# Attention with relative-position tables: the tables of a unit's two heads side by side and loaded in one transfer, queries as one run per partition

## The chip, the cores and the metric

The kernel runs on one core of one Trainium2 chip. The metric is the device time of one execution in microseconds. Before the change it is 1325.63 us, the median of three runs (1324.44 to 1329.54). A profile of one execution comes with it. Its engines are called PE (TensorE, matrix multiplication), DVE (VectorE), ACT (ScalarE), POOL (GpSimd) and SP (SyncE, which in this kernel issues most of the transfers); each issues its instructions in order, and the transfers that it issues form a queue of their own.

## The reference, cut to what matters

One layer over 2048 tokens (a grid of 32 rows by 64 columns) of width 1024. One in-projection makes the inputs of two branches, whose outputs lie beside each other and go through one out-projection.

```python
def hybrid_mixer(h, w_in, b_in, conv_w, conv_b, rpb, ml_norm_w, w_out):
    proj = h @ w_in + b_in
    (na_q, na_k, na_v, na_z, ml_q, ml_k, ml_v, ml_o, ml_z,
     i_f, f_f, i_b, f_b) = jnp.split(proj, split_idx, axis=-1)
    na_out = neighbourhood_attention(na_q, na_k, na_v, rpb) * jax.nn.silu(na_z)
    qk = jax.nn.silu(centred_short_conv(jnp.concatenate([ml_q, ml_k], axis=-1), conv_w, conv_b))
...
    # attention: each of 8 heads, each query: 8 rows x 16 columns of keys around it
    bias = rpb[:, dy[:, None, :, None], dx[:, None, :, None]]
    s = jnp.einsum('bhrcd,bhrjkd->bhrcjk', qg, kg).astype(jnp.float32) + bias[None]
    s = jnp.where(col_mask[:, None, :], s, -jnp.inf)
    p = jax.nn.softmax(s.reshape(B, NA_HEADS, rows, GRID_W, kh * GRID_W), axis=-1).reshape(s.shape)
    o = jnp.einsum('bhrcjk,bhrjkd->bhrcd', p, vg)
...
    return jnp.concatenate([na_out, ml_out], axis=-1) @ w_out
...
    # the layer
    h = rmsnorm(h_res, norm_w[l]) * (1.0 + scale[:, None, :]) + shift[:, None, :]
    h_res = h_res + gate[:, None, :] * y
    return rmsnorm(h_res, final_norm_w).astype(x.dtype)
```

The second branch is a bidirectional mLSTM of 4 heads, whose queries and keys pass the short convolution. The bias depends only on where a key lies relative to its query, and on the edges of the grid.

## The kernel before, in words

Everything is float32. A weight or an activation that goes through PE is split into a high and a low part, and a product is three matmuls (high by high, low by high, high by low). The work lies in stages one after the other:

- the start and the token blocks (to about 329 us): the norm, the values of both branches, the gates and decays of the mLSTM;
- the convolution stage, `conv_blocks` (329 to 519 us): the keys and queries of the mLSTM, four weight blocks of eight tiles each. A tile is 24 matmuls on PE into PSUM; ACT evicts it to a tile `u` (L891, four buffers); DVE convolves `u` into a tile `acc` in five instructions (L926, L928, five buffers); ACT applies SiLU (L930); SP stores `acc` to `d_ck` (L933). For keys, PE also transposes `acc` (L939, `kt`), ACT scales the result into `stk` (L941), and SP stores it (L943). Between tiles the generator `gated_out` prepares the out-projection's weights: SP loads a piece `wraw` (L854), DVE multiplies it by the gate (L861), SP stores it to `d_wo` (L862);
- the queries and keys of the attention (L986, PE's `pq`) and the mLSTM (to about 960 us);
- phase 2, the attention and the out-projection (to the end).

**The bias tables** are made by transfers alone. `tables_begin` fills the small tensors `d_e` in DRAM with a large number, `tables_columns` copies the bias of each column into them (L648, 48 transfers), `table_fills` fills the tables `d_t`, and `tables_rows` (L670) copies eight rows of `d_e` for each of eight grid rows into `d_t`, DRAM to DRAM, on SP. There are nine tables, three kinds of patch rows by three kinds of patch columns, with eight `tables_rows` copies each, 72 in all. `conv_blocks` calls `tables_rows` three times at the head of each of its first three weight blocks; each copy takes the eight heads as its first dimension.

**Phase 2** goes by units. The grid is cut into 16 patches of 8 rows by 16 columns (128 queries), and a unit is a patch with two of its heads: 64 units, taken two at a time. For a unit PE multiplies queries and keys (L1477), DVE adds the table and takes the minimum along the row in one instruction per head (L1485), ACT takes the exponent (L1486), DVE normalises (L1497), PE transposes the weights (L1505), ACT copies them out of PSUM (L1507), and PE multiplies them with the values (L1520). The out-projection's matmuls (L1565) lie between. A unit's tables lie in SBUF in `tabs`, two places of two tiles; neighbouring units of like patches share a place, and when a unit is the last user of its place, its minimum is followed by the load of the next unit's table, per head:

```python
                    if u in follows:
                        load_tab(follows[u], j)
```

`load_tab` (L1449) issues on SP, but for the first two units on POOL; `load_q` (L1392) loads the queries of two units, which were stored to `d_qna` in the stage before (L1025 and what follows).

**What sets the order.** Outside phase 2's hand-written schedule a scheduler orders each engine's instructions by its own estimate of when they are ready. So a change of a transfer's shape can move others.

## Time and profile before

| what | value |
|---|---|
| time, median of three runs | 1325.63 us (1324.44 to 1329.54) |
| span of the profiled execution | 1326.9 us |
| PE busy | 1294.6 us, 98% |
| DVE, ACT, POOL busy | 59%, 41%, 17% |
| SP's queue q1, share of 16 DMA engines over the span | 50.7% |
| start and token blocks, PE busy | 323.6 of 329 us |
| convolution stage (329 to 519 us), PE busy | 186.2 of 190 us, DMA share 0.64 |
| attention's queries and keys, mLSTM (519 to 960 us), PE busy | 436.9 of 441 us, DMA share 0.63 |
| phase 2 (960 to 1327 us), PE busy | 347.9 of 367 us, DMA share 0.74 |

The profiled execution's own time is its span, 1326.9 us, 1.3 us above the median of the runs. Rows of the timeline give start, duration, engine, line, instruction, output and inputs, and in brackets the idle time ahead of it with what ended it. On SP a row is an issue: its duration is the time SP took to hand the transfer over, not the transfer's. `x24` means that 24 such rows in a row are shown as one. A row of the table by windows gives the window, its length, the busy time of PE, PE's weight loads, DVE, ACT and POOL with the number of instructions, PE's granted clock (1.00 is full speed), the busy share of the 16 DMA engines and what they moved in GB/s.

### The profile page before, as it was taken

Reading aid. Unit: us, or ns where it says so; the run is one execution under the profiler, and the core shown is the slowest. Engines: PE = TensorE matmul, PEld = TensorE weight load, DVE = VectorE, ACT = ScalarE, POOL = GpSimd, SP = SyncE. Lnnn points to the kernel's source line nnn. Section 1 sums busy time; section 2 is a strip of 40 time slices with the busy share of each in tenths; the row PEclk is TensorE's granted clock in tenths of the full one; section 3 lists DMA queues with packets and bytes.
Section 4 is the critical chain, followed back from the end, with each engine's and each line's share of the span. In section 5 each row is a group of like instructions: output and inputs, shape, how many; then the busy total and the mean of one; then the engine's idle time right before and its main releaser. Section 6 shows DMA issues by size and latency. Waiting matters only on the chain. (4 is left out here: it accounts for less than half of the span.)

```text
span 1326.9 us, 23404 instructions
## 1 busy us (share of the span) xinstructions
PE 1294.6 (98%) x8330; PEld 1115.4 (84%) x8330; DVE 779.6 (59%) x2406; ACT 542.8 (41%) x1184; POOL 225.1 (17%) x280
## 2 busy tenths in 40 slices
PE   9999999999999999999999999999999999999996
PEld 8899999999878787888888888888777778778785
DVE  5754452112455559176768878767547576666663
ACT  5643324543222323123324323333356555565551
POOL 0243103331000000012212002121202211212211
PEclk9999999999999999999999999999999999999999
DMA  9998657998267685545756866746689977868871
GB/s 325 323 281 180 169 141 171 214 244 217 82 149 208 142 209 165 159 120 167 204 165 196 254 187 204 237 141 188 198 256 239 212 184 190 195 175 194 195 186 48
DMA packets 240487, 255.91 MB, mean 193 GB/s; under 512 B 31079, under 2 KB 200295, under 8 KB 240371
## 3 DMA queue, kind: packets, MB, share of 16 engines
q1 hardware_dynamic: 157006, 182.98, 50.7%
q0 software_dynamic: 20496, 36.21, 11.2%
q10 hardware_dynamic: 62868, 35.22, 9.6%
q8 instruction: 66, 1.08, 0.4%
q14 instruction: 51, 0.41, 0.1%
HBM read 169.81 MB, written 92.72 MB: 198 GB/s over the span
## 5 line engine op out<-in xcount | busy, mean ns | idle before, releaser
L986 PE MATMUL pq<-hhi,whi_a 128*128 128x512 f32 x512 | 208.2, 407 | 0.8 <-ACT u L891 0.8
L986 PE MATMUL pq<-hlo,whi_a 128*128 128x512 f32 x512 | 208.4, 407 | 0.0
L986 PE MATMUL pq<-hhi,wlo_a 128*128 128x512 f32 x512 | 206.7, 404 | 0.0
L986 PEld LDWEIGHTS pq<-hhi,whi_a 128*128 128x128 f32 x512 | 96.8, 189 | 17.8 <-ACT u L891 1.3
L986 PEld LDWEIGHTS pq<-hhi,wlo_a 128*128 128x128 f32 x512 | 96.8, 189 | 16.3
L986 PEld LDWEIGHTS pq<-hlo,whi_a 128*128 128x128 f32 x512 | 96.7, 189 | 16.0 <-issue 0.5
L1507 ACT ACTIVATE pt<-pT 96x384 f32<-96x384 f32 (+3 forms) x128 | 65.8, 514 | 86.7 <-PE pT L1505 84.0
L1486 ACT ACTIVATE pbuf<-pbuf,mn 128x480 f32<-128x480 f32 (+5 forms) x128 | 76.0, 594 | 53.0 <-DVE mn L1485 53.0
L960 POOL TENSOR_TENSOR wlo_a<-rawq,whi_a 128x1024 fp32r<-128x1024 f32 x19 | 45.8, 2409 | 296.1 <-ACT whi_a L959 263.7
L1565 PE MATMUL y<-hhi,whi_a 128*128 128x512 f32 x256 | 91.4, 419 | 0.5 <-ACT whi_a L1535 0.5
L1565 PE MATMUL y<-hhi,wlo_a 128*128 128x512 f32 (+1 forms) x272 | 90.7, 399 | 0.2 <-ACT y L1572 0.2
L1485 DVE CUSTOM_DVE_ANT_0 pbuf<-pS,tab 128x480 f32<-128x480 f32 (+5 forms) x128 | 62.9, 540 | 39.1 <-PE pS L1477 32.1
L1230 ACT ACTIVATE num<-px,gtile 128x129 f32<-128x129 f32 x120 | 38.3, 366 | 111.3 <-PE px L1225 86.5
L1505 PEld LDWEIGHTS pT<-ident,pbuf 128*128 128x128 f32 (+2 forms) x416 | 51.0, 137 | 29.6 <-issue 9.9
L618 DVE TENSOR_TENSOR stvo<-pvo,brow 128x256 f32<-128x256 f32 x64 | 26.6, 422 | 83.1 <-PE pvo L548 65.7
L1505 PE MATMUL pT<-ident,pbuf 128*128 128x128 f32 (+2 forms) x416 | 67.3, 275 | 8.2 <-DVE pbuf L1497 6.8
L546 PE MATMUL pvo<-whi_b,hhi 128*128 128x256 f32 x256 | 72.6, 284 | 0.0
L548 PE MATMUL pvo<-whi_b,hlo 128*128 128x256 f32 x256 | 72.1, 281 | 0.0
L547 PE MATMUL pvo<-wlo_b,hhi 128*128 128x256 f32 x256 | 72.0, 281 | 0.0
L1249 POOL TENSOR_TENSOR hm<-hm,ck 128x128 f32<-128x128 f32 x64 | 26.5, 414 | 252.9 <-DVE hm L1248 223.9
L833 ACT ACTIVATE dec<-dec,gtile 128x128 f32<-128x128 f32 x128 | 42.7, 393 | 53.6 <-POOL dec L826 50.8
L581 DVE TENSOR_TENSOR stv<-pv,brow 128x256 f32<-128x256 f32 x32 | 12.4, 421 | 74.4 <-DMA d_vna<-stv 43.4
(302 smaller groups left out, 3408.3 us busy)
## 6 DMA issues: line engine op xcount, KB each, us to landing
ck<-d_ck SPq DMA_DIRECT2D x64, 384.5 KB
rawq<-in_w_main_dram SPq DMA_DIRECT2D x28, 512.0 KB
raw<-in_w_main_dram SPq DMA_DIRECT2D x20, 512.0 KB
d_ck<-stvo SPq DMA_DIRECT2D x16, 514.0 KB
kv<-d_ck SPq DMA_DIRECT2D x64, 128.5 KB
wada<-in_w_ada_dram SPq DMA_DIRECT2D x32, 256.0 KB
dec<-d_mneg SPq DMA_DIRECT2D x32, 256.0 KB
d_ck<-dec ACTq DMA_DIRECT2D x32, 256.0 KB
```

The source lines that it names most:

```text
L546: nc.tensor.matmul(ps, lhi(k), rhi(k), start=(k == 0), stop=False)
L547: nc.tensor.matmul(ps, lhi(k), rlo(k), start=False, stop=False)
L548: self.mark = nc.tensor.matmul(ps, llo(k), rhi(k), start=False, stop=(k == KT - 1))
L833: nc.scalar.activation(t[:, o, :], t[:, o, :], AF.Exp, bias=self.cols["g"][:, d, h, c : c + 1])
L960: (eng or nc.gpsimd).tensor_tensor(lo[:, :, cs], raw, hi[:, :, cs].bitcast(F32), ALU.subtract)
L986: self.mark = nc.tensor.matmul(patch_ps(ps) if patch else ps, w, self.htok(h, g, k, patch), start=(k == 0 and n == 0), stop=(k == KT - 1 a ...
L1230: nc.scalar.activation(num[:, d, :], px[:, d, :], AF.Copy, scale=self.cols["inter"][:, d, h, c : c + 1])
L1485: nc.vector.tensor_tensor_reduce(pt[:, :nk], ps, tabs[place[u]][j][:, :nk], 1.0, 3e38, ALU.add, ALU.min, mn)
L1486: nc.scalar.activation(pt[:, :nk], pt[:, :nk], AF.Exp, bias=mn, scale=-1.0, accum_out=sums[:, j : j + 1])
L1505: nc.tensor.transpose(ps[:cs, i, :], U[u][j][:, i * cs : (i + 1) * cs], self.ident)
L1507: nc.scalar.activation(t[:cs, :nch, :], ps[:cs, :nch, :], AF.Copy)
L1565: nc.tensor.matmul(y, m[:, k, :], w[k][:, cs], start=(k == 4 and n == 0), stop=(k == 3 and n == 2))
```

## The change

Three layouts change, in DRAM and in SBUF.

- `d_e` and `d_t`, which held the 8 heads outermost, hold the 4 head pairs outermost; the two heads of a pair lie beside each other in a row. The copies of L648 and L670 follow: their access pattern begins with 4 instead of 8, and its second dimension is twice as long. Bytes and runs of each copy are the same.
- A unit's two tables are one SBUF tile of 960 columns instead of two of 480, and `load_tab` loads both in one transfer. It is issued once, behind the second head's minimum, where before each head's minimum was followed by its own load. SP issues 52 such transfers instead of 104, POOL 2 instead of 4.
- `d_qna` holds the queries of two units so that a partition reads one run of 2 KB instead of two of 1 KB. Their stores write runs of 512 bytes as before.

```diff
--- before.py
+++ after.py
@@ -98,7 +98,7 @@
         self.d_mneg = d.tile([P, CH], F32, name="d_mneg")
         self.d_zna = d.tile([16, P, 4, P], F32, name="d_zna")
         self.d_zml = d.tile([16, P, 4, P], F32, name="d_zml")
-        self.d_qna = d.tile([2, 2, 16, P, 2, P], F32, name="d_qna")
+        self.d_qna = d.tile([2, 16, P, 2, 2, P], F32, name="d_qna")
         self.d_kna = d.tile([2, 512, T], F32, name="d_kna")
         self.d_mix = d.tile([16, P, 4, P], F32, name="d_mix")
         self.d_wo = d.tile([KT, P, D], F32, name="d_wo")
@@ -106,9 +106,9 @@
         self.d_gate = d.tile([1, D], F32, name="d_gate")
         self.d_rneg = d.tile([NH, 15, 31], F32, name="d_rneg")
         nks = [24, 32, 24]
-        self.d_e = [d.tile([NH, 16, 15, nks[t]], F32, name=f"d_e{t}") for t in range(3)]
+        self.d_e = [d.tile([NH // 2, 16, 2, 15, nks[t]], F32, name=f"d_e{t}") for t in range(3)]
         nrs = [11, 15, 12]
-        self.d_t = [[d.tile([NH, P, nrs[r] * nks[t]], F32, name=f"d_t{r}{t}") for t in range(3)] for r in range(3)]
+        self.d_t = [[d.tile([NH // 2, P, 2, nrs[r] * nks[t]], F32, name=f"d_t{r}{t}") for t in range(3)] for r in range(3)]
 
     def constants(self):
         nc, c = self.nc, self.const
@@ -634,7 +634,7 @@
         nc.sync.dma_start(self.d_rneg.rearrange("h a b -> (h a) b"), r)
         for e in self.d_e:
             n = e.shape[-1] * 15 // 2
-            dst = e.rearrange("h c a k -> (h c) (a k)").rearrange("p (j n) -> p j n", j=2)
+            dst = e.rearrange("h c e a k -> (h c e) (a k)").rearrange("p (j n) -> p j n", j=2)
             nc.sync.dma_start(dst, self.big[:, :n].unsqueeze(1).broadcast_to([P, 2, n]))
 
     def tables_columns(self, ct):
@@ -645,7 +645,7 @@
             c = c0 + i
             start = min(max(c - 8, 0), GRID_W - 16)
             dx = start - c + 15
-            nc.sync.dma_start(self.d_e[ct][:, i, :, start - k0 : start - k0 + 16], self.d_rneg[:, :, dx : dx + 16])
+            nc.sync.dma_start(self.d_e[ct][:, i, :, :, start - k0 : start - k0 + 16].rearrange("h e a k -> h (e a) k"), self.d_rneg.rearrange("(h e) a k -> h (e a) k", e=2)[:, :, dx : dx + 16])
 
     def table_fills(self):
         nc = self.nc
@@ -653,7 +653,7 @@
             for rt in range(3):
                 t = self.d_t[rt][ct]
                 n = t.shape[-1]
-                dst = t.rearrange("h q k -> (h q k)").rearrange("(p j k) -> p j k", p=P, j=16)
+                dst = t.rearrange("h q e k -> (h q e k)").rearrange("(p j k) -> p j k", p=P, j=16)
                 nc.sync.dma_start(dst, self.big[:, : n // 2].unsqueeze(1).broadcast_to([P, 16, n // 2]))
                 yield
 
@@ -668,8 +668,8 @@
             dy = start - row + 7
             j0 = (start - PR_R0[pr]) * nk
             nc.sync.dma_start(
-                t[:, r * 16 : (r + 1) * 16, j0 : j0 + 8 * nk],
-                self.d_e[ct][:, :, dy : dy + 8, :].rearrange("h c a k -> h c (a k)"),
+                t[:, r * 16 : (r + 1) * 16, :, j0 : j0 + 8 * nk].rearrange("h q e n -> h (q e) n"),
+                self.d_e[ct][:, :, :, dy : dy + 8, :].rearrange("h c e a k -> h (c e) (a k)"),
             )
 
 
@@ -1022,7 +1022,7 @@
                 for e, part in enumerate((hv, lv)):
                     src = part.bitcast(F32).rearrange("p (a q) -> p a q", a=4)
                     if kind == "q":
-                        dst = self.d_qna[e, ct // 2, 4 * g : 4 * g + 4, :, ct % 2].rearrange("a p q -> p a q")
+                        dst = self.d_qna[ct // 2, 4 * g : 4 * g + 4, :, e, ct % 2].rearrange("a p q -> p a q")
                     else:
                         dst = self.d_kna[e, ct * P : (ct + 1) * P, g * GT : (g + 1) * GT].rearrange("p (a q) -> p a q", a=4)
                     late.append((dst, src))
@@ -1389,7 +1389,7 @@
             if 2 * i >= NU:
                 return
             b, c0 = units[2 * i][0], min(units[2 * i][1], units[2 * i + 1][1])
-            (nc.gpsimd, nc.gpsimd, nc.scalar, nc.sync)[min(i, 3)].dma_start(qs[i % 3].bitcast(F32), self.d_qna[:, c0 // 2, b].rearrange("e p c q -> p e c q"))
+            (nc.gpsimd, nc.gpsimd, nc.scalar, nc.sync)[min(i, 3)].dma_start(qs[i % 3].bitcast(F32), self.d_qna[c0 // 2, b])
 
         def load_v(b, most=4, queue=nc.gpsimd):
 
@@ -1434,7 +1434,7 @@
             L[b]["x"] = [x[:, 512 * i : 512 * i + 512] for i in range(2)]
             L[b]["row"] = x
 
-        tabs = [[p.tile([P, 480], F32, name=f"tab{i}{j}") for j in range(2)] for i in range(2)]
+        tabs = [p.tile([P, 960], F32, name=f"tab{i}") for i in range(2)]
         place, follows, user = [], {}, {}
         for u, (b, ct) in enumerate(units):
             same = [w for w in (u - 1, u - 3) if w >= 0 and units[w][1] == ct and units[w][0] != b and kind(units[w][0]) == kind(b)]
@@ -1443,10 +1443,11 @@
                 follows[user.get(place[u], -1 - place[u])] = u
             user[place[u]] = u
 
-        def load_tab(u, j):
+        def load_tab(u):
             b, ct = units[u]
             nk = geo[b][4]
-            (nc.gpsimd if u < 2 else nc.sync).dma_start(tabs[place[u]][j][:, :nk], self.d_t[PR_T[b // 4]][PC_T[b % 4]][2 * ct + j])
+            src = self.d_t[PR_T[b // 4]][PC_T[b % 4]][ct].rearrange("q e k -> q (e k)")
+            (nc.gpsimd if u < 2 else nc.sync).dma_start(tabs[place[u]][:, : 2 * nk], src)
 
         def load_w(k):
             (nc.gpsimd if k < 4 else nc.sync).dma_start(wolo[k].bitcast(F32), self.d_wo[k])
@@ -1482,11 +1483,11 @@
                 for j, ps in enumerate(made[u]):
                     pt = pbuf[(2 * u + j) % 4]
                     mn = few.tile([P, 1], F32, tag="mn", bufs=4, name=f"mn_{u}_{j}")
-                    nc.vector.tensor_tensor_reduce(pt[:, :nk], ps, tabs[place[u]][j][:, :nk], 1.0, 3e38, ALU.add, ALU.min, mn)
+                    nc.vector.tensor_tensor_reduce(pt[:, :nk], ps, tabs[place[u]][:, j * nk : (j + 1) * nk], 1.0, 3e38, ALU.add, ALU.min, mn)
                     nc.scalar.activation(pt[:, :nk], pt[:, :nk], AF.Exp, bias=mn, scale=-1.0, accum_out=sums[:, j : j + 1])
                     pts.append(pt)
-                    if u in follows:
-                        load_tab(follows[u], j)
+                if u in follows:
+                    load_tab(follows[u])
                 U[u] = (pts, sums)
 
         def normalised(u):
@@ -1616,8 +1617,7 @@
 
         for i in (0, 1):
             load_q(i)
-            for j in range(2):
-                load_tab(follows.pop(-1 - i), j) if j else load_tab(follows[-1 - i], j)
+            load_tab(follows.pop(-1 - i))
         self.close()
         pss = ExitStack()
         pS = self.pool(pss, "pS", bufs=4, space=PSUM)
```

SP around the second run of table copies, in the convolution stage (`d_t_76`, `d_t_79`, `d_t_82` are three of the tables, `raw` the next weights; the stores of `stk` and `acc` belong to the tiles at work). Before:

```order
L207 DMA raw_1_4322<-in_w_main_dram 128x1024
L670 DMA d_t_76<-d_e_73 8x16x256 x8
L670 DMA d_t_79<-d_e_73 8x16x256 x8
L670 DMA d_t_82<-d_e_73 8x16x256 x8
L943 DMA d_ck<-stk_1_4381 128x4x128
L933 DMA d_ck<-acc_k_2_4312 128x4x128
L854 DMA wraw_4392<-in_w_out_dram 128x512
```

The same place after the change:

```order
L207 DMA raw_1_4322<-in_w_main_dram 128x1024
L670 DMA d_t_76<-d_e_73 4x32x256 x8
L670 DMA d_t_79<-d_e_73 4x32x256 x8
L670 DMA d_t_82<-d_e_73 4x32x256 x8
L943 DMA d_ck<-stk_1_4381 128x4x128
L933 DMA d_ck<-acc_k_2_4312 128x4x128
L854 DMA wraw_4392<-in_w_out_dram 128x512
```

The place of the 24 copies is the same, and so are the stores behind them; only the shape of the copies differs. At the first run it is otherwise. SP there before the change:

```order
L670 DMA d_t_78<-d_e_72 8x16x192 x2
L586 DMA d_vna<-stv_3_3814 128x4x256
L670 DMA d_t_81<-d_e_72 8x16x192 x8
L847 DMA gate<-d_gate 128x1024
```

and with the change:

```order
L586 DMA d_vna<-stv_3_3814 128x4x256
L670 DMA d_t_75<-d_e_72 4x32x192 x3
L670 DMA d_t_78<-d_e_72 4x32x192 x8
L670 DMA d_t_81<-d_e_72 4x32x192 x8
L847 DMA gate<-d_gate 128x1024
```

Nineteen copies now stand in one piece ahead of the load of `gate`, where eight stood; the eleven others stood between the stores of the stage before.

PE in the convolution stage, a piece of the difference (`kt` are the transposes of the keys, `pc` the tiles of 24 matmuls):

```order
-L939 MATMUL kt_1_4564<-ident,acc_k_1_4480 128x128 x4
+L939 MATMUL kt_1_4376<-ident,acc_k_1_4262 128x128 x4
 L546 MATMUL pc_1_1_4584<-hhi_104,whi_b 128x512
 L547 MATMUL pc_1_1_4584<-hlo_105,whi_b 128x512
+L548 MATMUL pc_1_1_4584<-hhi_104,wlo_b 128x512
+L546 MATMUL pc_1_1_4584<-hhi_104,whi_b 128x512
+L547 MATMUL pc_1_1_4584<-hlo_105,whi_b 128x512
+L939 MATMUL kt_2_4423<-ident,acc_k_2_4312 128x128 x4
```

Five transposes, `kt_1_4376` to `kt_1_4564`, stand some four tiles later than they did. Elsewhere PE's order is as before.

SP in phase 2, at the change from one table to the next (`qs` are queries). Before:

```order
L1449 DMA tab_10051<-d_t_75 128x264
L1449 DMA tab_10052<-d_t_75 128x264
L1449 DMA tab_10049<-d_t_75 128x264
L1449 DMA tab_10050<-d_t_75 128x264
L1392 DMA qs_10044<-d_qna 128x2x256
L1449 DMA tab_10051<-d_t_76 128x352
```

After:

```order
L1450 DMA tab_10050<-d_t_75 128x528
L1450 DMA tab_10049<-d_t_75 128x528
L1392 DMA qs_10044<-d_qna 128x512
L1450 DMA tab_10050<-d_t_76 128x704
```

Two transfers of twice the width stand where four stood.

## The prediction

> **What bounds the kernel now.** I read the page first: the share of each engine, then the queues and the chain of waits.
>
> ```profile
> span 1326.9 us, 23404 instructions
> PE 1294.6 (98%) x8330; PEld 1115.4 (84%) x8330; DVE 779.6 (59%) x2406; ACT 542.8 (41%) x1184; POOL 225.1 (17%) x280
> q1 hardware_dynamic: 157006, 182.98, 50.7%
> ```
>
> TensorE (PE) is busy for 98% of the span. A gain can only come out of its 32 us of idle time, and whatever stops PE is paid in full: nothing behind the stop runs faster to make up for it. Queue q1, SyncE's, carries the tables and nearly everything else. So two questions decide: which of PE's idle time hangs on tables, and whether PE must now wait somewhere for a transfer that this change makes slower.
>
> For the first, the list of waits (engine, line, releaser: us in total, times, longest) and PE's rows behind the normalised weights in phase 2:
>
> ```profile
> PE pT L1505 <- DVE pbuf L1497: 6.8, 6, 2.0
> DVE pbuf L1485 <- DMA tab<-d_t: 6.8, 8, 1.6
> ...
> 1003.55 0.44 PE L1505 MATMUL pT<-ident,pbuf 128*120 128x128 f32 x1 [1.88 <-DVE pbuf L1497]
> 1055.27 0.30 PE L1505 MATMUL pT<-ident,pbuf 128*128 128x128 f32 x1 [1.59 <-DVE pbuf L1497]
> 1150.54 0.30 PE L1505 MATMUL pT<-ident,pbuf 128*128 128x128 f32 x1 [2.01 <-DVE pbuf L1497]
> 1233.61 0.29 PE L1505 MATMUL pT<-ident,pbuf 128*96 128x128 f32 x1 [0.55 <-DVE pbuf L1497]
> 1253.79 0.30 PE L1505 MATMUL pT<-ident,pbuf 128*120 128x128 f32 x1 [0.59 <-DVE pbuf L1497]
> ```
>
> VectorE's minimum (L1485) waits eight times for a table, 6.8 us. Four of PE's waits lie right behind such waits, at 1055, 1150, 1233 and 1253: 1.59 + 2.01 + 0.55 + 0.59 = 4.74 us. The wait at 1003 does not; no late table stands ahead of it. 4.74 us is the most that earlier tables can give.
>
> For the second, how the tables come to lie in memory. tables_rows (L670) copies from DRAM to DRAM on SyncE, in three runs during the convolution stage. SyncE's rows (start, duration of the run of issues), then VectorE and PE in that stage:
>
> ```profile
> 329.83 5.39 SPq L670 DMA_DIRECT2D d_t<-d_e  x8
> 370.87 6.26 SPq L862 DMA_DIRECT2D d_wo<-wraw  x2
> 392.83 19.17 SPq L670 DMA_DIRECT2D d_t<-d_e  x24
> 412.10 0.40 SPq L943 DMA_DIRECT2D d_ck<-stk  x1
> 412.83 0.38 SPq L933 DMA_DIRECT2D d_ck<-acc_k  x1
> 451.57 19.24 SPq L670 DMA_DIRECT2D d_t<-d_e  x24
> 471.42 0.45 SPq L933 DMA_DIRECT2D d_ck<-acc_k  x1
> ...
> 419.61 0.49 DVE L926 TENSOR_SCALAR acc_k<-u,cw 128x512 f32<-128x512 f32 x1
> 446.01 0.69 DVE L861 TENSOR_TENSOR wraw<-wraw,gate 128x512 f32<-128x512 f32 x1 [12.34 <-DMA wraw<-in_w_out_dram]
> 477.89 0.49 DVE L926 TENSOR_SCALAR acc_q<-u,cw 128x512 f32<-128x512 f32 x1 [8.17 <-DMA d_ck<-acc_k]
> ...
> 452.34 0.66 PE L939 MATMUL kt<-ident,acc_k 128*128 128x128 f32 x4 [2.06 <-ACT acc_k L930]
> ```
>
> The row at 477.89 is the one to notice: before any change, the convolution on VectorE stands for 8.17 us until the store of an earlier acc tile has landed, and that store was issued at 471.42, right behind 24 table copies. There are five acc buffers, so a late store stops the convolution, then the u tiles, then PE. What the engines of the DMA do meanwhile stands in the table by window (us, busy times, granted clock, share of the 16 DMA engines, GB/s):
>
> ```profile
> 398.00:412.00 14.00, 14.00 (x66) 11.34 (x65) 8.12 (x17) 5.19 (x7) 0.00 (x0) 1.00 0.55 184
> 444.00:456.00 12.00, 9.56 (x45) 7.33 (x44) 7.37 (x15) 4.83 (x9) 0.00 (x0) 1.00 1.14 217
> 462.00:470.00 8.00, 8.00 (x37) 6.46 (x36) 4.62 (x10) 2.73 (x5) 0.00 (x0) 1.00 0.55 155
> ```
>
> While only table copies run, the share is 0.55 in both runs; with transfers of 128 rows beside them it is 1.14. Yet the copies are queued without a gap. So they keep some half of the 16 engines busy and leave the rest idle. Their access pattern begins with 8, the heads.
>
> **The change part by part.**
>
> *The copies into the tables (L670, and L648 ahead of it).* Bytes, runs and number stay (72 copies of 128 runs of 768 or 1024 bytes), but the pattern now begins with 4, the head pairs, instead of 8. No row shows a large copy that begins with 4, so I bound it. One end is no change. The other is that a copy spreads over as many engines as its first dimension counts: 8 of 16 is 0.50, near the 0.55 of the rows (other transfers are among them), and 4 would give half the rate. I take the halving, because two rows point at the first dimension: 8 gives 0.55, 128 gives 1.14. Then the second run, 24 copies of 128 KB at 184 GB/s or some 17 us, takes 17 us more, and the third, 24 of 96 KB at 155 GB/s, 15.2 us more.
>
> The Trainium skill, page "DMA: Bandwidth & Descriptors", section "Why a DMA increments its semaphore by 16 and not by 1", says how many engines a transfer uses: the largest number up to 16 that divides the slowest dimension of both its patterns. By that rule the copies go from 8 engines to 4. It speaks against this change; this trace bears out its 8 (0.55), and no row here shows its 4.
>
> *What stands behind the copies.* The run of 329.83 grows from 8 copies to 19, since the scheduler has moved eleven of them behind the earlier stage. 5.39 us for 8 becomes some 5.39 x 19/8 x 2 = 25.6 us; it ends near 356 instead of 335. What is behind it on SyncE is weight loads whose products are stored at 370 (L862), and acc stores with five buffers to spare: 0. If that cover were short, each us past 370 would cost one. The columns (L648) go the same way:
>
> ```profile
> d_e<-d_rneg SPq DMA_DIRECT2D x48, 7.5 KB
> ```
>
> 48 x 7.5 KB is 0.36 MB, a seventh of a long run, spread over the token stage, and only table copies read it: 0.
>
> The second run delays the stores of 412.10 and 412.83 by 16 to 17 us, and the convolution of 419.61, which needs an acc buffer, to 436 (16.3 later). VectorE then has its wait of 12.34 us at 446.01, for a weight load; this cover takes 12.3, and 16.3 - 12.3 = **4.0 us** reach PE, at the transposes of 447 to 452 and the tiles behind them. Bounds: 0 (the scheduler's later transposes wait less), and 7 if the weight loads behind the copies are as late as the stores.
>
> The third run has no such cover.
>
> ```profile
> 483.94 0.67 ACT L891 ACTIVATE u<-pc,bcol 128x512 f32<-128x512 f32 x1
> ...
> 513.43 0.69 ACT L891 ACTIVATE u<-pc,bcol 128x512 f32<-128x512 f32 x1 [4.16 <-PE pc L548]
> 516.09 0.71 ACT L930 ACTIVATE acc_q<-acc_q,cb 128x512 f32<-128x512 f32 x1
> 519.01 0.69 ACT L891 ACTIVATE u<-pc,bcol 128x512 f32<-128x512 f32 x1 [2.21 <-PE pc L548]
> 519.75 0.50 PE L986 MATMUL pq<-hhi,whi_a 128*128 128x512 f32 x1 [0.84 <-ACT u L891]
> ```
>
> The convolution of 477.89 moves to 493.1. The eviction of 483.94 needs a u tile that this convolution frees and moves to 499.1. PE makes a tile every 5.6 us (513.43 to 519.01) and holds four of them, so the tile due at 519.01 - 5 x 5.57 = 491.2 starts at 499.8: a wait of 8.6 us. The stage ends with VectorE's chain, which is 15.2 us late by then: its last step but a few, 516.09, comes at 531.3, and the next stage's first matmul, 519.75 now, at about 532: **12.3 us** in all. Bounds: 10.3, if VectorE regains two us from waits it had for stores, and 16 if the whole delay reaches PE with one eviction more.
>
> *PE's moved transposes.* Five groups of kt stand four tiles later. One had waited:
>
> ```profile
> 394.79 0.44 PE L939 MATMUL kt<-ident,acc_k 128*128 128x128 f32 x2 [1.27 <-ACT acc_k L930]
> ```
>
> With four tiles of 5.6 us ahead this wait goes: **-1.3 us**.
>
> *The clock.* PE's granted clock after stops of nearly 2 us:
>
> ```profile
> 1002.00:1004.00 2.00, 0.45 (x3) 0.48 (x4) 1.97 (x9) 1.92 (x8) 0.56 (x1) 0.84 1.00 188
> 1004.00:1008.00 4.00, 4.00 (x15) 3.19 (x15) 2.08 (x5) 2.34 (x4) 0.00 (x0) 0.65 1.05 372
> ```
>
> After the stop at 1003 the clock was 0.84 for 2 us and 0.65 for 4: 0.32 + 1.40 = 1.7 us lost. A stop of 8.6 us should meet this once: **+1.7**, between 0 (after 1.59 us at 1055 the clock stayed) and 3.4 (two stops).
>
> *The tables in phase 2.* One transfer per unit instead of two halves the packets and doubles each. The load is issued one minimum later for the first head.
>
> ```profile
> 1041.74 1.81 SPq L1449 DMA_DIRECT2D tab<-d_t  x4
> 1051.48 0.52 DVE L1485 CUSTOM_DVE_ANT_0 pbuf<-pS,tab 128x352 f32<-128x352 f32 x1 [0.79 <-DMA tab<-d_t]
> 1053.63 0.53 DVE L1485 CUSTOM_DVE_ANT_0 pbuf<-pS,tab 128x352 f32<-128x352 f32 x1 [1.62 <-DMA tab<-d_t]
> ...
> tab<-d_t POOLq DMA_DIRECT2D x4, 144.0 KB, 6.3
> ```
>
> On free queues a table lands in 6.3 us; at 1041.74 it took 9.7 to 10.4, so other queues cost some 3.8 us. If packets take turns, twice the packet halves this: 1.9 us. The later issue takes back 0.5 (one L1485). Of waits of 1.59, 2.01, 0.55 and 0.59 that leaves 0.2, 0.6, 0 and 0: **-4.0 us**. Bounds -4.74 and +1 (no gain from the packets, two waits longer by 0.5). The queries' longer runs stand on no path: their load does not occur among VectorE's or PE's waits. 0.
>
> **Sum**, against the profiled span: 1326.9 + 4.0 + 12.3 - 1.3 + 1.7 - 4.0 = 1339.6. The span lies 1.3 us above the median of the runs (1325.63), so in the metric **1338.3 us**.
>
> **The rivals.**
>
> *R1, the copies do not slow down* (the engines, not the first dimension, set the 0.55; or issuing does). For it: an issue row of 24 in 19.17 us is 0.8 us each, which could be SyncE's own pace. Against: eight took 5.39 us, 0.67 each, so it slows as the queue fills. Then only -1.3 and -4.0 stay: 1326.9 - 5.3 - 1.3 = 1320.3, no longer than before. It decides from the point where a copy that begins with 4 holds the share at 0.5.
>
> *R2, halved but covered*: the delay is 17 us, but the stage has buffers (five acc, four u, four PSUM tiles) that start full. Only part of the third run, some 6 us with no dip, reaches PE: 1325.63 + 6 - 5.3 = 1326.3. Against it stands the 8.17 at 477.89: the buffers are used up already.
>
> *R3, the stops add up*: run 2 costs 7, run 3 16, two dips 3.4, the tables give 4: 1325.63 + 7 + 16 + 3.4 - 1.3 - 4.0 = 1346.7. For it: the wait of 12.34 is itself for a load on SyncE, which is late too, so it may be no cover.
>
> *R4, tables land later*: both heads wait for the second minimum and for the longer transfer. As the forecast without its -4.0 and with +1: 1343.3.
>
> **How the numbers follow.** Chances: the forecast 0.52, R3 0.20, R1 0.15, R2 0.10, R4 0.03. The forecast's own range is 1331 to 1345 (with 0, 10.3 and no dip: 1338.3 - 4.0 - 2.0 - 1.7 = 1330.6; with 7 and 16: 1338.3 + 3.0 + 3.7 = 1345.0). The range for 8 in 10 is **1324 to 1349**: it leaves out most of R1 and the tail of R3. A difference of 0.5%, 6.6 us, is about what a measurement of this kernel can tell from none. Slower than 1332.3: nearly all of the forecast, R3 and R4, 0.50 + 0.20 + 0.03 = **0.73**. Faster than 1319.0: a third of R1, **0.05**. Within: the rest, **0.22**.
>
> **What will show it.** In the windows of the two long runs the DMA share should be near 0.28 instead of 0.55, and last until some 17 and 15 us later. VectorE's wait for the store of acc in the third run should grow from 8.17 to over 20 us, PE should show a wait of about 8 us near 491 to 500, and its first pq matmul should start near 530. In phase 2 VectorE's waits for tab should be under 3 us in total, with as much PE time from the first table to the end otherwise. The prediction is wrong if the share stays at 0.55, or if it halves and the pq matmul still starts before 523.

## The result, and the profile after

The changed kernel takes 1343.84 us in the median of four runs (1339.01 to 1345.09), the kernel before 1325.67 us in the same comparison. The ratio is 1.0108, with a 95% interval of 1.0084 to 1.0133: slower, beyond the half per cent that this kernel's measurement can tell from none. (The medians alone give 1.0137, the fastest runs of the two kernels 1.0110.) The profiled execution, 1337.2 us of span, is the fastest of the four. Its time in the metric is 1339.01 us, 1.8 us above its span; by that the profiled execution of the kernel before, 1326.9 us of span, was a run of about 1328.7 us, near the slowest of its set. So the two profiles show less of the change than the medians do: 10.3 us against 18.2.

The page of the changed kernel: span, engines, SyncE's queue. Behind it the waits of PE and VectorE that matter (engine, line, releaser: us in total, times, longest us). Lines from L1450 on have moved by one.

```profile
span 1337.2 us, 23272 instructions
PE 1296.3 (97%) x8330; PEld 1116.4 (83%) x8330; DVE 780.4 (58%) x2406; ACT 541.6 (41%) x1184; POOL 224.6 (17%) x278
q1 hardware_dynamic: 145326, 182.97, 48.2%
...
PE pc L546 <- ACT u L891: 7.6, 1, 7.6
PE kt L939 <- ACT acc_k L930: 4.3, 3, 2.1
PE pT L1506 <- DVE pbuf L1498: 4.3, 4, 1.9
PE pq L986 <- ACT u L891: 2.0, 1, 2.0
DVE pbuf L1486 <- DMA tab<-d_t: 6.7, 7, 2.1
```

The bytes of the queue are the same (182.97 MB, before 182.98), its packets fewer by 11,680. A wait is there that was not there before: 7.6 us in one piece, for the eviction to `u`. The windows of the two long runs of copies (us, busy time of PE, PE's weight loads, DVE, ACT and POOL, granted clock, DMA share, GB/s):

```profile
402.00:424.00 22.00, 22.00 (x107) 18.01 (x106) 8.53 (x18) 8.19 (x12) 0.00 (x0) 1.00 0.28 92
463.00:484.00 21.00, 21.00 (x93) 17.01 (x92) 5.35 (x12) 3.62 (x6) 0.00 (x0) 1.00 0.28 80
```

The share has gone from 0.55 to 0.28 and the rate from 184 and 155 GB/s to 92 and 80, half within a few per cent. What follows from it, in the timelines of SyncE, VectorE and PE:

```profile
330.20 20.53 SPq L670 DMA_DIRECT2D d_t<-d_e  x19
392.62 33.43 SPq L670 DMA_DIRECT2D d_t<-d_e  x24
427.57 1.24 SPq L933 DMA_DIRECT2D d_ck<-acc_k  x1
455.67 29.70 SPq L670 DMA_DIRECT2D d_t<-d_e  x24
486.70 0.93 SPq L933 DMA_DIRECT2D d_ck<-acc_k  x1
...
435.54 0.49 DVE L926 TENSOR_SCALAR acc_k<-u,cw 128x512 f32<-128x512 f32 x1 [17.67 <-DMA d_ck<-acc_k]
494.45 0.49 DVE L926 TENSOR_SCALAR acc_q<-u,cw 128x512 f32<-128x512 f32 x1 [22.11 <-DMA d_ck<-acc_k]
...
442.10 0.65 PE L939 MATMUL kt<-ident,acc_k 128*128 128x128 f32 x4 [2.09 <-ACT acc_k L930]
501.29 0.80 PE L546 MATMUL pc<-hhi,whi_b 128*128 128x512 f32 x1 [7.64 <-ACT u L891]
533.08 0.50 PE L986 MATMUL pq<-hhi,whi_a 128*128 128x512 f32 x1 [2.05 <-ACT u L891]
```

Read from the top, this is a chain: SyncE's run of copies ends 14 us and 15 us later than before, the store of `acc` behind it is issued that much later, VectorE's convolution stands for that store (22.11 us, 8.17 before), and PE stands 7.64 us at 501. The first `pq` matmul comes at 533.08 instead of 519.75. That is 13.3 us; from there to the end the changed kernel takes 804.1 us where the kernel before took 807.2, so 3.0 us come back in these two profiles, and the spans differ by 10.3.

### The profile page after: what moved, and what is told of

The parts are those of the page before. It is cut to its first block, busy times and chain, and to the rows that moved or that the text cites. A ratio compares the mean times of both kernels' runs of the same rounds, so it can differ in the third digit from the quotient of the medians.

```text
span 1337.2 us, 23272 instructions
## 1 busy us (share of the span) xinstructions
PE 1296.3 (97%) x8330; PEld 1116.4 (83%) x8330; DVE 780.4 (58%) x2406; ACT 541.6 (41%) x1184; POOL 224.6 (17%) x278
## 3 DMA queue, kind: packets, MB, share of 16 engines
q1 hardware_dynamic: 145326, 182.97, 48.2%
## 4 chain that ended last, share of the span: by engine, by line
PE 64%; DMA 14%; issue 7%; DVE 6%; SPq 5%; ACT 2%; POOL 1%; ACTq 0%; POOLq 0%; DVEq 0%
PE pq L986 20%; PE y L1566 12%; SPq L670 4%; PE pvo L546 3%; PE pO L1521 3%; PE pvo L548 3%; PE pvo L547 3%; PE pvo L601 3%; PE pT L1506 3%; DMA d_ck<-dec 3%; PE pS L1478 2%; DMA tab<-d_t 2%; DMA dec<-d_mneg 2%; PE pi L1227 2%; PE px L1225 2%
## 5 line engine op out<-in xcount | busy, mean ns | idle before, releaser
L1506 PEld LDWEIGHTS pT<-ident,pbuf 128*128 128x128 f32 (+2 forms) x416 | 50.6, 136 | 27.0 <-issue 6.9
L1506 PE MATMUL pT<-ident,pbuf 128*128 128x128 f32 (+2 forms) x416 | 66.8, 273 | 5.9 <-DVE pbuf L1498 4.3
L546 PE MATMUL pc<-hhi,whi_b 128*128 128x512 f32 x128 | 51.6, 403 | 7.6 <-ACT u L891 7.6
```

The source lines that it names most:

```text
L546: nc.tensor.matmul(ps, lhi(k), rhi(k), start=(k == 0), stop=False)
L1506: nc.tensor.transpose(ps[:cs, i, :], U[u][j][:, i * cs : (i + 1) * cs], self.ident)
```

## The experiments

The experiments were made in three sets of runs, in which the kernel before takes 1331 to 1332 us in the median, not 1325.7; every ratio is to the kernel before in the same set. Each run has one profile.

**The same copies in another order.** The kernel before, with the first two dimensions of the table copies exchanged.

```diff
             nc.sync.dma_start(
-                t[:, r * 16 : (r + 1) * 16, j0 : j0 + 8 * nk],
-                self.d_e[ct][:, :, dy : dy + 8, :].rearrange("h c a k -> h c (a k)"),
+                t[:, r * 16 : (r + 1) * 16, j0 : j0 + 8 * nk].rearrange("h q n -> q h n"),
+                self.d_e[ct][:, :, dy : dy + 8, :].rearrange("h c a k -> c h (a k)"),
             )
```

> The kernel before, with one edit: the table copies (L670) take the same runs in another order, the 16 grid columns as the first dimension of the access pattern and the 8 heads as the second. Layouts, bytes, runs and number of copies stay. Theory (the first dimension sets how many DMA engines a copy uses): in the runs of copies the DMA share rises from 0.55 to about 1.0, VectorE's wait of 8.17 us for a store of acc behind the third run goes, PE keeps at most its short waits there: first pq matmul at 516 to 520 instead of 519.75, time 1322 to 1326 us. Rival (SyncE's issuing or DRAM sets the pace of the copies): share stays near 0.55, SyncE's run of 24 stays near 19 us, time as before, 1325.6.

Measured: 1330.07 us, ratio 0.9988 (0.9973 to 1.0002). A window of this kernel, with the share in the last column but one, and the timelines of SyncE, VectorE and PE:

```profile
446.00:456.00 10.00, 8.51 (x39) 7.03 (x40) 9.27 (x20) 4.99 (x8) 0.00 (x0) 1.00 0.62 145
...
437.51 20.02 SPq L670 DMA_DIRECT2D d_t<-d_e  x24
458.26 0.45 SPq L933 DMA_DIRECT2D d_ck<-acc_k  x1
477.76 0.48 DVE L926 TENSOR_SCALAR acc_q<-u,cw 128x512 f32<-128x512 f32 x1 [0.89 <-DMA d_ck<-acc_q]
297.40 0.38 PE L546 MATMUL pv<-whi_b,hhi 128*128 128x256 f32 x1 [1.96 <-DVE stv L581]
521.40 0.51 PE L986 MATMUL pq<-hhi,whi_a 128*128 128x512 f32 x1 [0.84 <-ACT u L891]
```

Half of the theory's expectations held. VectorE's long wait for a store is gone. But the copies do not go faster: 145 GB/s and 20.02 us for 24 issues, where the kernel before had 155 GB/s and 19.24. So with 16 as the first dimension something else sets their pace, and the row that stays the same is SyncE's, 0.8 us per copy. The wider spread does not buy speed. Why the wait for the store went is not shown by this run: the scheduler has also moved the copies. The second run no longer stands in one piece, the third begins at 437.51 instead of 451.57, and the store behind it is issued at 458.26, some 13 us earlier than before (471.42), while the convolution comes at the same time. PE gains nothing in the end, since copies now stand in the token stage, where PE stands 1.96 us for the `stv` stores.

**The same layouts, copies of four heads.** The kernel before with each table copy cut in two.

```diff
-            nc.sync.dma_start(
-                t[:, r * 16 : (r + 1) * 16, j0 : j0 + 8 * nk],
-                self.d_e[ct][:, :, dy : dy + 8, :].rearrange("h c a k -> h c (a k)"),
-            )
+            for h0 in (0, 4):
+                nc.sync.dma_start(
+                    t[h0 : h0 + 4, r * 16 : (r + 1) * 16, j0 : j0 + 8 * nk],
+                    self.d_e[ct][h0 : h0 + 4, :, dy : dy + 8, :].rearrange("h c a k -> h c (a k)"),
+                )
```

> The kernel before, with one edit: each table copy (L670) is cut into two of four heads each, so 144 copies that begin with 4, with the old layouts, the old loads and the same runs. Theory: the share in the runs of copies falls to about 0.28 as in the changed kernel, the stores behind land some 15 us late, first pq matmul at 530 to 535, time 1337 to 1342 us (phase 2 keeps its waits for tables). Rival (the pairs' layout in DRAM, not the first dimension, made the copies slow): share stays near 0.55, first pq near 520, time 1325 to 1329.

Measured: 1352.02 us, ratio 1.0150 (1.0126 to 1.0175). Windows, VectorE and PE of this kernel:

```profile
410.00:428.00 18.00, 18.00 (x86) 14.76 (x85) 7.12 (x14) 4.36 (x6) 0.00 (x0) 1.00 0.28 93
472.00:490.00 18.00, 18.00 (x80) 14.58 (x79) 1.71 (x6) 1.99 (x3) 0.00 (x0) 1.00 0.28 80
...
500.56 0.49 DVE L927 TENSOR_SCALAR acc_q<-u,cw 128x512 f32<-128x512 f32 x1 [21.75 <-DMA d_ck<-acc_k]
507.89 0.80 PE L546 MATMUL pc<-hhi,whi_b 128*128 128x512 f32 x1 [7.77 <-ACT u L892]
540.83 0.50 PE L987 MATMUL pq<-hhi,whi_a 128*128 128x512 f32 x1 [2.75 <-ACT u L892]
```

The old layout, the old loads and the same bytes, and the changed kernel's stage all over: 0.28, 80 GB/s, 21.75 us on VectorE, 7.77 on PE. The pairs in memory are not needed for it. One more rival is left, since this kernel also issues twice as many copies: 48 in 35.8 us are 0.75 us each, near the 0.8 that 24 take before the change, so that SyncE's issuing could be the limit here. The trace's records of the single packets speak against it: in both windows SyncE's queue has at least four under way for 99% of the time, four or five for some nine tenths, as in the changed kernel's two windows, where 24 copies take 1.39 and 1.24 us each; in the kernel before it has at least eight for 96% or more. In the experiment before this one, from 447 to 456 us, the number goes up and down between 1 and 17. So it is the first dimension of the copies. The size was missed; the first `pq` was expected at 530 to 535 and came at 540.83, where the kernel with the queries' layout alone, last below, has it at 520.46.

**The layouts and copies as changed, loads as before.** Each head's table again in a tile of its own, loaded behind its own minimum.

```diff
-        tabs = [p.tile([P, 960], F32, name=f"tab{i}") for i in range(2)]
+        tabs = [[p.tile([P, 480], F32, name=f"tab{i}{j}") for j in range(2)] for i in range(2)]
...
-            src = self.d_t[PR_T[b // 4]][PC_T[b % 4]][ct].rearrange("q e k -> q (e k)")
-            (nc.gpsimd if u < 2 else nc.sync).dma_start(tabs[place[u]][:, : 2 * nk], src)
+            (nc.gpsimd if u < 2 else nc.sync).dma_start(tabs[place[u]][j][:, :nk], self.d_t[PR_T[b // 4]][PC_T[b % 4]][ct, :, j])
...
-                if u in follows:
-                    load_tab(follows[u])
+                    if u in follows:
+                        load_tab(follows[u], j)
```

> The changed kernel, but each head's table is loaded by itself behind its own minimum, into four tiles, as before the change; the layouts and the copies stay as changed. Theory (the one transfer per unit took PE's waits for tables away): convolution stage as in the changed kernel (first pq near 533), phase 2 with 4 to 5 us of PE waits behind late tables again, so 3 to 4 us above the changed kernel: 1341 to 1347 us by the span. Rival (those waits went because phase 2 runs at another phase against the other queues, or the loads made no difference): within 1 us of the changed kernel.

Measured: 1359.54 us, ratio 1.0205 (1.0181 to 1.0228). To read it one needs the changed kernel beside a kernel before of about the same time; it was run again in the second set:

> The changed kernel once more, on the chip of the three kernels beside it, since its runs lay 1339 to 1345 us, 6 us apart, and the one with a profile was the fastest. Theory (the copies of L648 and L670 that begin with 4 also make stores of the token stage late, more in some runs than in others): the profile shows PE waits for the stv stores (L546) before 329 us, 0.7 us in the first profile, 3 to 8 us in a slower run, with a dip of the clock behind. Rival (only the clock differs): those waits stay under 1 us and the convolution stage or the clock make the difference.

Measured: 1356.08 us, ratio 1.0187 (1.0168 to 1.0207). So the changed kernel loses more here than in the first comparison. Its timelines show where, VectorE first, then PE (the `kt` rows of 4.38 and 2.46 us are two of four):

```profile
299.02 1.09 DVE L581 TENSOR_TENSOR stv<-pv,brow 128x256 f32<-128x256 f32 x3 [15.98 <-DMA d_vna<-stv]
...
299.50 0.58 PE L546 MATMUL pv<-whi_b,hhi 128*128 128x256 f32 x1 [5.53 <-DVE stv L581]
315.10 0.39 PE L546 MATMUL pv<-whi_b,hhi 128*128 128x256 f32 x1 [1.25 <-DVE stv L581]
453.26 1.12 PE L939 MATMUL kt<-ident,acc_k 128*128 128x128 f32 x4 [4.38 <-ACT acc_k L930]
468.16 0.66 PE L939 MATMUL kt<-ident,acc_k 128*128 128x128 f32 x4 [2.46 <-ACT acc_k L930]
514.26 0.79 PE L546 MATMUL pc<-hhi,whi_b 128*128 128x512 f32 x1 [5.86 <-ACT u L891]
547.09 0.51 PE L986 MATMUL pq<-hhi,whi_a 128*128 128x512 f32 x1 [3.34 <-ACT u L891]
```

PE stands 6.8 us in the token stage for VectorE, which stands for the store of `stv` behind copies on the same queue; in the first profile of the changed kernel that stop was 0.67 us. The theory named 3 to 8 us, and it is there. But the larger part of the difference lies in the convolution stage: from its first matmul to the first `pq` it takes 209.1 us here, 204.0 in the first profile of the same kernel and 191.0 before the change. With one load per head the same stop is 7.5 us, so a comparison of whole times says little about phase 2. The waits do: at the four places that the prediction named (L1505 or L1506, some 30 us later here) PE's waits add up to 1.22 + 0.98 + 0.79 + 0.38 = 3.37 us with one load per head, and to 0.49 + 1.01 = 1.50 with one per unit, the same copies in both. The times lie 3.5 us apart, as expected, but they are of two sets and the intervals of the ratios overlap.

**Position outermost.** The changed kernel with `d_e` as [16, 8, 15, nk] and `d_t` as [128, 8, n]; a unit's two tables still lie side by side.

```diff
-        self.d_e = [d.tile([NH // 2, 16, 2, 15, nks[t]], F32, name=f"d_e{t}") for t in range(3)]
+        self.d_e = [d.tile([16, NH, 15, nks[t]], F32, name=f"d_e{t}") for t in range(3)]
...
-        self.d_t = [[d.tile([NH // 2, P, 2, nrs[r] * nks[t]], F32, name=f"d_t{r}{t}") for t in range(3)] for r in range(3)]
+        self.d_t = [[d.tile([P, NH, nrs[r] * nks[t]], F32, name=f"d_t{r}{t}") for t in range(3)] for r in range(3)]
...
-                t[:, r * 16 : (r + 1) * 16, :, j0 : j0 + 8 * nk].rearrange("h q e n -> h (q e) n"),
-                self.d_e[ct][:, :, :, dy : dy + 8, :].rearrange("h c e a k -> h (c e) (a k)"),
+                t[r * 16 : (r + 1) * 16, :, j0 : j0 + 8 * nk],
+                self.d_e[ct][:, :, dy : dy + 8, :].rearrange("c h a k -> c h (a k)"),
```

> The changed kernel with the grid position outermost in d_e and d_t (16 or 128 first, then 8 heads): a unit's two tables still lie side by side and load in one transfer, and each table copy begins with 128. Theory: share about 1.0 in the runs of copies, no stop of PE in the convolution stage (first pq at 516 to 520), and phase 2's gain of 3 to 4 us stays: 1318 to 1323 us, faster than both kernels. Rival (the layout in pairs costs something by itself, or the loads from rows that lie eight heads apart are slower): 1326 or more.

Measured: 1329.34 us, ratio 0.9988 (0.9970 to 1.0006). Its twin, with one load per head into tiles of their own and all else the same:

> The kernel with the grid position outermost (copies that begin with 128, all in runs as before), but each head's table loaded by itself behind its own minimum into its own tile; beside it stands the same kernel with one load per unit from an earlier run (0.9988 of the kernel before, 3.1 us of PE waits behind the normalised weights). Theory (the one load per unit takes PE's waits for late tables away): those PE waits are 6 to 8 us again, time 2 to 4 us more, ratio 1.000 to 1.003. Rival (the waits went for another reason): 3 to 4 us of waits, ratio 0.998 to 0.9995.

Measured: 1330.05 us, ratio 0.9993 (0.9978 to 1.0008). All rows of PE behind late normalised weights after 1040 us, of the kernel with one load per unit, and of its twin:

```profile
1059.54 0.52 PE L1506 MATMUL pT<-ident,pbuf 128*128 128x128 f32 x3 [0.46 <-DVE pbuf L1498]
1079.74 0.63 PE L1506 MATMUL pT<-ident,pbuf 128*128 128x128 f32 x4 [0.19 <-DVE pbuf L1498]
1236.23 0.50 PE L1506 MATMUL pT<-ident,pbuf 128*96 128x128 f32 x3 [0.28 <-DVE pbuf L1498]
```

```profile
1059.85 0.52 PE L1505 MATMUL pT<-ident,pbuf 128*128 128x128 f32 x3 [0.48 <-DVE pbuf L1497]
1154.27 0.52 PE L1505 MATMUL pT<-ident,pbuf 128*128 128x128 f32 x3 [1.28 <-DVE pbuf L1497]
1238.11 0.51 PE L1505 MATMUL pT<-ident,pbuf 128*96 128x128 f32 x3 [1.31 <-DVE pbuf L1497]
1258.26 0.51 PE L1505 MATMUL pT<-ident,pbuf 128*120 128x128 f32 x3 [0.59 <-DVE pbuf L1497]
```

0.93 us against 3.66. Counted in the same way over all profiles (where a kernel runs later, from that much later on), the six kernels with one load per head have 2.9 to 5.4 us of such waits and the eight profiles with one load per unit 0.9 to 2.8: the one load per unit does what its place in the change suggests, though less in some profiles than in others. The 13 us of loss are gone as well, with the pairs still side by side. But no gain can be shown in time: the twins' ratios, of two sets, have overlapping intervals, and from the first `pq` to the end the kernels with one load per head take 806.0 to 810.5 us, those with one per unit 804.1 to 810.7. In the profile, what is won in phase 2 against the kernel before (4.74 - 0.93 us) meets 3.2 us that PE now loses in the token stage, as in the first experiment.

**The columns' copies.** The changed kernel with 30 instead of 4 as the first dimension of L648 alone.

```diff
-start - k0 : start - k0 + 16].rearrange("h e a k -> h (e a) k"), self.d_rneg.rearrange("(h e) a k -> h (e a) k", e=2)[:, :, dx : dx + 16])
+start - k0 : start - k0 + 16].rearrange("h e a k -> (e a) h k"), self.d_rneg.rearrange("(h e) a k -> (e a) h k", e=2)[:, :, dx : dx + 16])
```

> The changed kernel with one edit: the 48 copies of columns (L648) take the same runs with 30 as the first dimension instead of 4. L670 stays with 4. Theory (L648 on few engines delays the token stage, L670 the convolution stage): PE's waits for stv before 329 us fall under 1 us, the convolution stage stays as in the changed kernel (first pq about 13 us later than before), time 0 to 6 us under the changed kernel's on this chip. Rival (L648 costs nothing): time as the changed kernel, within 2 us.

Measured: 1359.09 us, ratio 1.0211 (1.0189 to 1.0232), no faster than the changed kernel. PE's waits before 329 us:

```profile
188.16 0.44 PE L713 MATMUL ps_c_w<-ident,wide 128*128 128x128 f32 x1 [4.35 <-DVE gtile L803]
314.37 0.58 PE L546 MATMUL pv<-whi_b,hhi 128*128 128x256 f32 x1 [2.54 <-DVE stv L581]
```

The stop for `stv` fell from 6.8 to 2.5 us, not under 1, and a stop of 4.35 us for the gate chain came in its stead, out of a new order of the instructions. The experiment doesn't decide. Beside it stands that the kernel with copies of four heads, whose L648 still begins with 8, has no stop for `stv` at all. The two paced kernels below tell more, since neither issues a table copy before the convolution stage. In the one whose columns' copies begin with 4, VectorE waits up to 12.2 us for the `stv` stores and PE stands 1.79 us; in the one whose columns' copies begin with 120 (heads and rows of a head in one), it is 4.7 us and PE does not stand. So the columns' copies have a part in the token stage's loss; how much of the 6.8 us is theirs stays open.

**The copies spread out.** If a backlog is what does the harm, slow copies that come three at a time should be harmless. The changed kernel, copies still beginning with 4, three per tile behind the tile's eviction; and the layout with the position outermost, paced in the same way:

```diff
+                    for _ in range(3):
+                        next(rows, None)
...
+            self.behind(copy, self.pace)
+            yield
```

> The changed kernel, the table copies (L670) still beginning with 4, but issued three per tile behind the eviction of that tile, in 24 tiles of the convolution stage, instead of 24 at a time. Theory (the stop comes from the backlog of a run of copies on few engines: three copies of 128 KB at 92 GB/s take 4.2 us of a tile's 5.6): no stop at the tile near 500, PE waits under 5 us in the convolution stage, first pq at 517 to 523, time 1320 to 1328. Rival (each slow copy holds the store behind it, so pacing spreads the loss and does not take it away): first pq past 528, time over 1335.

> The layout with the grid position outermost (copies that begin with 128) and the pacing of three copies per tile together, with the one load per unit. Theory: no PE waits for stv before 329 us (none of the copies stands there any more), at most 3 us in the convolution stage, phase 2's gain of 3 us kept: 1319 to 1323 us where the kernel before takes 1326, in proportion on a slower chip (0.995). Rival (the gain in phase 2 is eaten by what the new order of the stage moves): 0.999 to 1.005.

Measured: 1359.22 us, ratio 1.0209 (1.0187 to 1.0231), and 1344.92 us, ratio 1.0105 (1.0085 to 1.0124). Both missed, for a reason of their own. VectorE and PE of the second, the one with copies that begin with 128 (in the first the same copy waited 17.39 us):

```profile
513.40 0.23 DVE L1064 COPY perm<-ident 128x128 f32<-128x128 f32 x1 [17.04 <-PE pc L548]
532.60 0.79 PE L988 MATMUL pq<-hhi,whi_a 128*128 128x512 f32 x1 [19.24 <-ACT u L891]
```

The scheduler had moved a copy of the next stage into the middle of VectorE's convolution; it waited there for PE's last tile, and the convolutions behind it with it. With that copy put behind the last convolution:

```diff
-        nc.vector.tensor_copy(self.perm.rearrange("p (a r k) -> p a r k", r=2, k=16), patch_order(self.ident))
+        self.behind(nc.vector.tensor_copy(self.perm.rearrange("p (a r k) -> p a r k", r=2, k=16), patch_order(self.ident)), self.conved)
```

> The changed kernel with its copies that begin with 4, issued three per tile, and the permutation's copy (L1064) behind the last convolution. Theory (a backlog of 24 copies on few engines makes the stop, so that spread over 24 tiles the same slow copies do little): PE waits of at most 6 us in the convolution stage, of which 3.8 at 479 for weights, first pq at 522 to 530, ratio 1.000 to 1.008. Rival (slow copies hold every store behind them and VectorE stays late): first pq past 535, ratio over 1.012.

> The kernel with copies that begin with 128 and are issued three per tile, with one edit: the copy of the permutation (L1064), which had moved into the middle of VectorE's convolution and waited 17.04 us there for PE's last tile, stands behind the last convolution, as in the kernel before. Theory (that one copy cost the 19 us; pacing on all engines takes the stop away): no PE wait over 2 us between 130 and 525 us, first pq at 515 to 521, phase 2's gain kept, ratio to the kernel before 0.992 to 0.998. Rival (the paced order makes the stage's end late in other ways too): ratio 1.000 to 1.008.

Measured, beginning with 4: 1341.78 us, ratio 1.0086 (1.0071 to 1.0100), first `pq` at 530.79. Beginning with 128: 1328.76 us, ratio 0.9984 (0.9966 to 1.0001), first `pq` at 517.12. PE's waits between 130 us and that matmul, in the first kernel (one more is of 1.79 us, for `stv`) and in the second:

```profile
475.96 0.79 PE L546 MATMUL pc<-hhi,whi_b 128*128 128x512 f32 x1 [3.56 <-ACT whi_b L211]
530.79 0.79 PE L988 MATMUL pq<-hhi,whi_a 128*128 128x512 f32 x1 [7.00 <-ACT u L891]
```

```profile
517.12 0.51 PE L988 MATMUL pq<-hhi,whi_a 128*128 128x512 f32 x1 [3.77 <-ACT u L891]
```

With the same slow copies, pacing takes the stop near 500 away; VectorE's longest wait for a store of `acc` in the stage is 3.32 us, and the stage takes 199.3 us where the changed kernel's two profiles have 204.0 and 209.1. The time lies between the theory's figures (at most 6 us of PE waits in the stage, a ratio to 1.008) and the rival's: 10.6 us and 1.0086. Its loss is half of the changed kernel's in the second set (1.0187), but hardly below the one of the first comparison (1.0108). So the backlog did a part of the harm, and not all of it: paced alike, the kernel with copies that begin with 128 takes 189.3 us for the stage, 10 us less. Slow copies still delay stores a little each, and 7.00 us are left at the stage's end. The other kernel has the earliest `pq` of all, but phase 2 keeps 2.8 us of waits for tables, and its time cannot be told from the kernel before.

**The queries alone.** The kernel before with the new layout of `d_qna`.

```diff
-        self.d_qna = d.tile([2, 2, 16, P, 2, P], F32, name="d_qna")
+        self.d_qna = d.tile([2, 16, P, 2, 2, P], F32, name="d_qna")
```

> The kernel before with the queries' new layout alone: one run of 2 KB per partition in a load instead of two of 1 KB. Theory: nothing waits for the queries, so ratio 0.999 to 1.001. Rival (half as many packets beside the tables lets these land earlier): PE's waits for late tables fall by 1 to 2 us, ratio 0.998 to 0.999.

Measured: 1331.90 us, ratio 1.0007 (0.9989 to 1.0025): nothing in time, as the theory had it. In its profile PE's waits behind late weights are 2.85 us instead of 4.74, which is what the rival named; but kernels with one load per head differ by as much from profile to profile (2.9 to 5.4 us), so this one profile decides nothing.

## Why the prediction was right

The direction, the mechanism and the place hold: slower, because the table copies keep a quarter instead of half of the DMA engines busy, in the convolution stage. That the number is near is luck in part. Forecast was 12.7 us more; the medians differ by 18.2 us, the two profiles by 10.3, and in the second set the same kernel takes 25.0 us more than the kernel before. Step by step:

- *The halving.* Forecast share 0.28; measured 0.28 in both runs, 92 and 80 GB/s for 184 and 155. The sentence cited from the Trainium skill (page "DMA: Bandwidth & Descriptors", section "Why a DMA increments its semaphore by 16 and not by 1") gives 4 engines here; this row now bears out its 4 as well, and the copies of four heads in the old layout bear it out apart from the change.
- *The delays.* The convolution of 419.61 was forecast at 436 and came at 435.54; that of 477.89 at 493.1, and came at 494.45. PE's stop was forecast at 8.6 us near 499.8 and was 7.64 at 501.29. The first `pq` was forecast at about 532 and came at 533.08. The third run's agreement has another make-up than the forecast: SyncE begins it 4.1 us later (455.67 for 451.57), because the second run had delayed what stands ahead of it, and takes 10.5 us longer over it (29.70 for 19.24), where the forecast had 15.2 us longer from the same start. The run of 330.20, forecast at 25.6 us, took 20.53 and cost PE nothing, as forecast.
- *What was counted twice.* The sum added 4.0 for the second run and 12.3 for the third, and 1.7 for the clock. The 12.3, read off the first `pq`, was taken as if the second run had delayed nothing. But what passes the cover of the second run is what makes the third begin 4.1 us late, so in the trace the delay of the first `pq` holds it already. In the first profile the whole stage is 13.0 us longer where the terms 4.0 + 12.3 - 1.3 + 1.7 give 16.7: all PE waits from the stage's start to `pq` add up to 14.0 us against 4.6 before, 9.5 more, and the clock takes the rest. The cover held as forecast: VectorE's instruction of 446.01 comes at 449.14, 3.1 us late, so 12.8 of the 15.9 us were absorbed, and PE's waits for `kt` are 4.3 us instead of 3.7. The gain of 1.3 at 394.79 was there, and went again at 442 to 455. In the second profile of the same kernel the cover did less: PE stands 7.8 us for `kt`, and the stage is 18.1 us longer.
- *The clock.* One dip was counted; there were two. Windows of the changed kernel cut to the dips, with the granted clock in the last column but two:

```profile
443.40:446.70 3.30, 3.24 (x11) 2.23 (x10) 3.30 (x9) 1.71 (x3) 0.00 (x0) 0.50 1.23 207
501.30:504.70 3.40, 3.40 (x8) 2.75 (x9) 3.40 (x10) 1.30 (x2) 0.00 (x0) 0.50 1.11 206
```

The clock was 0.50 for 3.3 us behind the stop of 2.09 us at 442, and for 3.4 us of work behind the stop of 7.64: about 1.7 us lost each time, 3.4 us in place of 1.7. So the price of a dip was right, and their number was not.

- *Phase 2.* Forecast -4.0, measured -3.0 between `pq` and the end in the first profile; this is not shown to be the tables' doing. The kernel before has a dip of the clock at 1003 there, 1.7 us, and the changed kernel has none; and in its second profile the same stretch takes 807.4 us, no less than the 807.2 before. What did happen is that from 1040 us on PE's waits behind late weights fell from 4.74 us to 1.00, and to 1.50 in the second profile. One of the signs named was wrong: VectorE's waits for tables were to fall under 3 us and stayed at 6.7 (7 of them, one of 2.1). PE stands behind two of them, 1.00 us in all, so most now cost nothing. The wait to read was PE's.
- *The step that failed* is the one that costed the token stage at nothing: "48 x 7.5 KB is 0.36 MB, a seventh of a long run, spread over the token stage, and only table copies read it: 0." It asked who reads the data and not which stores stand behind the copies on SyncE. Those are the stores of `stv`, and VectorE waited up to 10.5 us for them before the change already, as the list of waits of the kernel before has it:

```profile
DVE stv L581 <- DMA d_vna<-stv: 43.4, 6, 10.5
```

  The columns' copies have also come nearer to these stores: in the changed kernel 23 of the 48 are issued after 204 us, before it the last was issued at about 201. PE's cover there was thin. In the first profile that cost 0.67 us, in the second 6.8, with a dip of the clock behind it. It may be a part of why the times of the changed kernel lie above its first profile; in the runs without a profile it can't be seen.
- *The rivals.* R1 (the copies do not slow down) fell with the share. Yet there may be something in its reason: with 16 first the copies got no faster, and SyncE's 0.8 us per copy is the row that stayed. R2 fell with the stop at 501. R3 (the stops add up, two dips, 1346.7, or 21.1 us more) came nearest after the forecast: its two dips were there, its 7 us for the second run were not in the first profile, and the median of 1343.84 lies between the two. In the second set, with 25.0 us more, 7.8 us of waits for `kt` and three dips in the stage, R3 was the nearer one.

## What to carry to other kernels

When a layout changes, write down the access pattern that every transfer then begins with, those in earlier stages too: of two patterns over the same bytes the one that begins with 4 ran at half the rate of the one that begins with 8, and cost 13 to 18 us in a stage that the change did not mean to touch. Cost a slower transfer by what is queued behind it on its engine as well as by who reads it. And where an order is a scheduler's, look for instructions that a new shape has moved on every engine: one copy of 0.2 us in the wrong place held VectorE for 17 us, and with it put right the next stage began 15 us earlier.

## What the runs showed of the hardware that was not expected

- The rate of the DRAM-to-DRAM copies of 768 bytes a run was 80 GB/s with 4 as the first dimension, 155 with 8, and 145 with 16. What stayed the same from 8 to 16, and with 128 too, was SyncE's 0.8 us per copy of 128 runs (19.24, 20.02 and 19.91 us for 24); that it sets the pace there is read from this, and was not tried by itself.
- In all the kept traces every dip of the granted clock was to 0.50. The 0.84 and 0.65 that the prediction reads after the stop at 1003 are means over windows that a dip fills in part; cut to the dip, the kernel before has:

```profile
1003.40:1006.70 3.30, 3.15 (x10) 2.58 (x11) 2.23 (x7) 1.96 (x4) 0.00 (x0) 0.50 1.02 359
```

  Stops of about 2 us bring a dip in some places and not in others: 1.88 us did here and 2.09 us did in the changed kernel at 442, while 2.06 us at 452 and 2.01 us at 1150 in the kernel before brought none:

```profile
1150.00:1154.00 4.00, 3.46 (x20) 2.96 (x21) 3.54 (x17) 2.18 (x8) 0.00 (x0) 1.00 1.03 165
```

- The same changed kernel lost 1.1% in one set of runs and 1.9% in another, where the kernel before differed by 0.4%. The two profiles differ in how long the stores of the token stage take beside the copies (9.2 us more than before up to the convolution stage, against 0.4), and in that stage itself (18.1 us more, against 13.0). What makes the same program differ so is not known.
